# Attention in 16 steps of two query tiles in a given order, parts of queries and keys made for 128 rows at once, and rearranged ends

## The chip, the cores and the metric

One NeuronCore of a Trainium2 chip runs the kernel. Its engines work from instruction streams of their own, each in order: PE (TensorE, matrix products and transposes), DVE (VectorE), ACT (ScalarE), POOL (GpSimd) and SP (SyncE, here used to issue DMAs). The time is that of the device for one execution, in microseconds; three runs of the kernel before gave 1841.4 (median), 1840.13 (lowest) and 1842.2 (highest).

## What is computed

A decoder trunk of two layers on one sequence of 512 tokens with 1024 features, all in float32. Cut to what matters:

```python
for l in range(2):
    x = x + 0.5 * swiglu(rms_norm(x, ffn1_norm[l]), ffn1_w_in[l], ffn1_w_out[l])
    h = rms_norm(x, mix_norm[l]) @ w_mix_in[l]
    (c_x, c_b, c_c, h_q, h_f, h_i, h_g, f_q, f_k, f_v, f_f) = split(h)
    y = concatenate([
        short_conv_mixer(c_x, c_b, c_c, conv_w[l]),              # 256 columns
        hgrn2_mixer(h_q, h_f, h_i, h_g, lower_bounds[l], ...),   # 256 columns, 4 heads
        fox_mixer(f_q, f_k, f_v, f_f, fox_f_bias[l], ...),       # 512 columns, 8 heads of 64
    ])
    x = x + y @ w_mix_out[l]
    x = x + 0.5 * swiglu(rms_norm(x, ffn2_norm[l]), ffn2_w_in[l], ffn2_w_out[l])

def fox_mixer(q, k, v, f_logit, f_bias, q_gain, k_gain):         # forgetting attention
    qh = rms_norm(heads(q), q_gain) * 64 ** -0.5
    kh = rms_norm(heads(k), k_gain)
    cum = cumsum(log_sigmoid(f_logit + f_bias))
    s = qh @ kh.T + (cum[:, None] - cum[None, :])                # causal mask: -1e30
    return softmax(s) @ heads(v)
```

The hidden width of the SwiGLU is 2816.

## The kernel before

Every float32 operand of a product is split into two parts of the type fp32r: hi, a rounded copy made on ACT, and lo, the remainder made on DVE (`parted`, L337 and L338). A product is then three matrix products: hi by hi (L349), hi by lo (L355), lo by hi (L356), which add up in one bank of PSUM (`mm3`). There are eight banks under four names: `mm` (3), `sc` (2), `pt` (2) and `po` (1).

`stream_steps` is the loop for a dense projection. It takes two rows of 128 weights at a time (a granule): `granule` has SP load them into a `st` buffer (two of these), ACT and DVE make hi and lo in an `hl` buffer (three of these, hi and lo in one), and PE runs the products of all banks. Casts that run ahead (`high_priority`) are put early in the order of ACT and DVE. `wide` splits the steps of a generator in two, so that other work can be recorded between two halves; with it the first granule is taken bank by bank, else row by row, and the last one is always taken bank by bank. A line recorded through `follow` keeps its place after the line of the same engine that was recorded so before it; everything else is placed by the scheduler.

The stages of a layer:

- `ffn` (first half): `cover` runs the first columns of the input projection in steps of two column blocks (`f` = 0, 2, 4) while normalisation and a planned order of half-size products follow, then the output projection over two halves `dg`. In layer 0 `open_x` brings x in: eight pieces of 256 KB, each loaded by SP (`load_x`, L1565), transposed on PE (L1568), scaled by the gain on ACT (`norm_part`, L426) and DVE (L427). `begin_norm` (L415) loads a gain as a tile of 128 rows and 8 columns. The constants are built on DVE (L209 to L270).
- `mix`: the input projection of the three mixers. `hgrn` runs as two generators (one for each pair of heads), each `yield` of which is followed by one dense half-step of `fox_qkv` (from the third on). After the loop `fox_decay` (eight products at L1358, then `negc` at L1363 on ACT and L1364 on DVE, two parts of 8 rows) is recorded, then what is left of `fox_qkv`, 24 products of V.
- The attention, `fox_attend`: 32 items (head, tile of 128 queries). `fox_prep` makes the operands of one head: QA holds hi and lo of the queries (64 rows each), QB hi and two rows of ones, KA hi twice, KB lo and the head's two rows of `negc`. It turns queries and keys together on PE (L1419), makes the parts by two ACT operations (L1422, L1423) and two DVE operations (L1426, L1430) over 64 rows, and copies two of them by DMA on SP (L1424, L1425) from the rows where they were made to those where they belong; KB's two rows come straight from `negc` in SBUF (L1415). `scores` runs three products for an item (L1446 to L1448, the last one adds the mask in bfloat16), the row maximum on DVE, the exponential on ACT. The item's weights are turned on PE (L1510), split, and multiplied with V (`values`, L1468) once for two items. `LOOK` = 3 items of scores stand ahead. `dense` gives the short convolution's projections (`conv`) and the output projection of the six row blocks that are ready (`most`); the set `BESIDE` says beside which items one dense step is recorded.
- After the attention the last two row blocks of the output projection (`order` puts them last), and the second `ffn`. In the last layer `turn_x` (L1531, L1536) turns x back to tokens ahead of the output projection, whose banks are added to it on DVE (L510) and stored (L514).

Of the kernel before, what the change touches and what calls it, by code (L numbers as in the profile page):

```python
# [22 lines left out]
LOOK, LAG = 3, 1  # L23

BESIDE = {0, 1, 2, 33} | {4 + (29 * n) // 20 for n in range(20)}
# [158 lines left out]
class Trunk:  # L184
# [35 lines left out]
    def build_consts(self, scratch):  # L220
# [38 lines left out]
        for l in range(1, 7):  # L259
            nc.vector.tensor_scalar(a, xf, scalar1=float(2 ** (l - 1)), scalar2=None, op0=ALU.is_ge)  # L260
# [22 lines left out]
    def table(self, name):  # L283

        p = self.nc.scalar.preload_act_table_set(name)
        for user in self.tab_users:
            self.tc.add_manual_dep(p.ins, user, NOSYNC, reason="table order")
        self.tab_users = []
        self.tab = p.ins.name
# [15 lines left out]
    def granule(self, parts, kk, ahead=True, skew=0, keep=False):  # L305

        nc = self.nc
        c = sum(ap.shape[1] for ap in parts)
        st = self.wp.tile([P, 1024], F32, tag="st", name=self.n("st"), bufs=2)
        s3 = st[:, : kk * c].rearrange("p (k c) -> p k c", k=kk)
        at = 0
        for ap in parts:
            w = ap.shape[1]
            nc.sync.dma_start(s3[:, :, at : at + w], ap.rearrange("(k p) c -> p k c", p=P))
            at += w
        with self.tc.high_priority() if ahead else ExitStack():  # L320
            hi, lo = self.parted(st[:, : kk * c], 1 if ahead else kk, skew, keep)
        h3, l3 = (a.rearrange("p (k c) -> p k c", k=kk) for a in (hi, lo))
        return [(h3[:, i, :], l3[:, i, :]) for i in range(kk)]

    def parted(self, src, pieces=1, skew=0, keep=False):
# [9 lines left out]
        for c in range(0, n, w):  # L335
# [3 lines left out]
            if pieces > 1 or keep:  # L339
                self.follow("a", a)  # L340
                self.follow("v", b)
        return hh, ll
# [21 lines left out]
    def stream_steps(self, jobs, parts_of, act, nk, mid=None, pre=None, deal=None, keep=False, wide=False):  # L364
# [12 lines left out]
        while k < nk:  # L377
            kk = min(2, nk - k)
            if callable(mid) and k == nk - 2:
                mid()  # L380
            if pre is not None:
# [4 lines left out]
            rows = self.granule(parts_of(k, kk), kk, pre is None, skew, deal is not None)  # L386
            end = k + kk == nk
            order = (
                [(job, j) for job in jobs for j in range(kk)]
                if end or wide and k == 0  # L390
                else [(job, j) for j in range(kk) for job in jobs]
            )
            for n, ((acc, cols, toks, *more), j) in enumerate(order):
                if pre is not None and n == len(order) // 2:
                    pre(k, True)
                if wide and n == len(order) // 2:
# [3 lines left out]
                first, last = k + j == 0 and not more, end and j == kk - 1  # L400
                if toks is None:
                    self.mm3(acc, hi[:, cols], lo[:, cols], ah, al, first, last, False, keep)
                else:
                    self.mm3(acc, ah[:, toks], al[:, toks], hi[:, cols], lo[:, cols], first, last)
# [7 lines left out]
    def begin_norm(self, gain_ap):  # L412
# [3 lines left out]
        self.sqacc = None  # L416

# [54 lines left out]
    def ffn(self, w_in, w_out, next_gain, covered, mean=None, begin=None, out=None):  # L472
# [5 lines left out]
        with tc.tile_pool(name=self.n("ffn"), bufs=1) as fp:  # L478
# [11 lines left out]
            if last:  # L490
                xs = self.turn_x()
            for dg in range(2):
# [7 lines left out]
                self.stream(  # L500
# [5 lines left out]
                )  # L506
                if last:
                    for i in range(4):
                        o = self.xo[dg * 4 + i]
                        nc.vector.scalar_tensor_tensor(  # L510
                            out=o, in0=banks[i], scalar=0.5, in1=xs[dg * 4 + i],
                            op0=ALU.mult, op1=ALU.add,
                        )
                        nc.sync.dma_start(out[0, spans[i], dg * T : (dg + 1) * T], o)  # L514
# [11 lines left out]
    def cover(self, fp, w_in, w_out, covered, mean, begin):  # L526
# [65 lines left out]
        for f in range(0, covered, 2):  # L592
            banks = self.next4()

            def parts(k, kk, f=f):
# [9 lines left out]
                None if opening else (lambda k, f=f: deal(2 * f + k // 2)), begin is None or f > 2,  # L605
            )
# [325 lines left out]
    def mix(self, l, w, w_out, conv_w, out_gain, q_gain, k_gain, f_bias, next_gain, logits):  # L932
# [3 lines left out]
        with tc.tile_pool(name=self.n("mix"), bufs=1) as mp:  # L936
# [23 lines left out]
            def features_steps(spans, banks, mid=None):  # L960
# [3 lines left out]
                    [(b, c, None) for b, c in zip(bs, FM2)], cols(*spans), self.xact, KD, mid  # L964
# [11 lines left out]
            def tokens(*spans):  # L976
# [4 lines left out]
                    self.xact, KD, wide=True,  # L981
# [3 lines left out]
            with tc.tile_pool(name=self.n("hg"), bufs=1) as hp:  # L985
# [60 lines left out]
                self.fox_decay(mp, zf)  # L1046
                for _ in dense:
                    pass
            with tc.tile_pool(name=self.n("at"), bufs=1) as ap_:
                self.tt, self.tb = "t", 3  # L1050
# [4 lines left out]

                def conv():
                    for i in range(2):
                        bx, bc = yield from features_steps(
                            [(C_X + i * P, P), (C_C + i * P, P)], ("mm", "mm")
                        )  # L1060
                        self.conv_in(ap_, i, bx, bc, inv2, cw)
                    bb = yield from features_steps([(C_B, 256)], ("mm", "mm"))
# [6 lines left out]
                def rows(k0, a, n):  # L1069
                    return lambda k, kk: [  # L1070
                        w_out[order[k0 + k] * P : (order[k0 + k] + kk) * P, a : a + n]
                    ]
# [7 lines left out]
                def most():  # L1080

                    for dg in range(4):
# [3 lines left out]
                            rows(0, 256 * dg, 256), act(0), 6,  # L1086
# [10 lines left out]
                for n, _ in enumerate(self.fox_attend(ap_, half, qkg)):  # L1097
                    if n in BESIDE:
                        next(g)
                    if n == max(BESIDE):  # L1100
                        next(g, None)
                self.ntog = 0
                for dg in range(2):
# [3 lines left out]
                        rows(6, 512 * dg, 512), act(6), 2,  # L1107
# [36 lines left out]
    def hgrn(self, l, pr, hp, z, q, q2, v, sg, og):  # L1144
# [42 lines left out]
        self.act(kd, kd, AF.Exp)  # L1187
        tb = self.bank("pt")
# [153 lines left out]
    def fox_decay(self, mp, zf):  # L1342
# [13 lines left out]
        for j in range(4):  # L1356
# [5 lines left out]
        self.negc = mp.tile([NH, 2, T], F32R, tag="negc", name=self.n("negc"))  # L1362
        nc.scalar.activation(self.negc[:, 0, :], cb[:NH, :], AF.Copy, scale=-1.0)  # L1363
        nc.vector.scalar_tensor_tensor(  # L1364
            out=self.negc[:, 1, :], in0=cb[:NH, :], scalar=-1.0, in1=self.negc[:, 0, :],
            op0=ALU.mult, op1=ALU.subtract,
        )

# [38 lines left out]
    def fox_prep(self, pool, h, qk, g):  # L1407
# [3 lines left out]

        nc = self.nc
        tl = lambda p, tag: pool.tile([p, T], F32R, tag=tag, name=self.n(tag), bufs=2)
        QA, QB, KA, KB = tl(P, "QA"), tl(66, "QB"), tl(P, "KA"), tl(66, "KB")
        nc.sync.dma_start(KB[64:66, :].bitcast(F32), self.negc[h : h + 1, :, :].bitcast(F32))  # L1415
        nc.gpsimd.memset(QB[64:66, :].bitcast(F32), 1.0)
        b = self.bank("pt")
        for i in range(4):
            nc.tensor.transpose(  # L1419
                b[:, i * P : (i + 1) * P], qk[:, i, h % 4].rearrange("p w d -> p (w d)"), self.ident  # L1420
            )
        nc.scalar.activation(QA[:64, :], b[:64, :], AF.Copy, scale=g[:64, :])  # L1422
        nc.scalar.activation(KA[64:, :], b[64:, :], AF.Copy, scale=g[64:, :])  # L1423
        nc.sync.dma_start(QB[:64, :].bitcast(F32), QA[:64, :].bitcast(F32))  # L1424
        nc.sync.dma_start(KA[:64, :].bitcast(F32), KA[64:, :].bitcast(F32))  # L1425
        nc.vector.scalar_tensor_tensor(  # L1426
            out=QA[64:, :], in0=b[:64, :], scalar=g[:64, :], in1=QA[:64, :],
            op0=ALU.mult, op1=ALU.subtract,
        )
        nc.vector.scalar_tensor_tensor(  # L1430
            out=KB[:64, :], in0=b[64:, :], scalar=g[64:, :], in1=KA[64:, :],
            op0=ALU.mult, op1=ALU.subtract,
        )
        return QA, QB, KA, KB

    def fox_attend(self, pool, half, g):
# [3 lines left out]
        tl = lambda tag, n: pool.tile([P, T], F32, tag=tag, name=self.n(tag), bufs=n)  # L1440

        def scores(ops, i):
            QA, QB, KA, KB = ops
            c, n = slice(i * P, (i + 1) * P), (i + 1) * P
            sb = self.bank("sc")
            nc.tensor.matmul(sb[:, :n], QA[:, c], KA[:, :n], start=True, stop=False)  # L1446
            nc.tensor.matmul(sb[:, :n], QB[:, c], KB[:, :n], start=False, stop=False)
            nc.tensor.matmul(sb[:, c], self.identb, self.maskb, start=False, stop=True)  # L1448
            s1 = lambda tag: pool.tile([P, 1], F32, tag=tag, name=self.n(tag), bufs=3)
            nm, rs = s1("nm"), s1("rs")  # L1450
            nc.vector.tensor_reduce(nm, sb[:, :n], axis=AX.X, op=ALU.max, negate=True)
            pb = tl("P", 3)
            self.act(pb[:, :n], sb[:, :n], AF.Exp, bias=nm, accum_out=rs)
            nc.vector.reciprocal(rs, rs)
            if i == 3:
                nc.scalar.activation(pb[:, :n], pb[:, :n], AF.Copy, scale=rs)
            else:
                nc.vector.tensor_scalar(pb[:, :n], pb[:, :n], scalar1=rs, scalar2=None, op0=ALU.mult)
            return pb

        def values(h, i, PH, PL):
            if i == 1:
                self.ob = self.bank("po")
            t0 = (i - 1) * P
            for j in range(i + 1):
                u = 1 if j == i else 0
                for part in (PH, PL):
                    nc.tensor.matmul(  # L1468
                        self.ob[:, t0 + u * P : t0 + 2 * P],
                        half[2][:, j, h].rearrange("p a d -> p (a d)"),  # L1470
                        part[:, j, u:, :].rearrange("p i t -> p (i t)"),
                        start=j == 0 and part is PH, stop=j == i and part is PL,
                    )
            if i < 3:
# [5 lines left out]
            ft = tl("t", self.tb)  # L1480
# [7 lines left out]
        late = []  # L1488
        items = [(h, i) for h in range(NH) for i in range(4)]
        prep = lambda h: self.fox_prep(pool, h, half[h // 4], g)  # L1490
        ops = {0: prep(0)}
        yield
        pb = {it: scores(ops[0], it[1]) for it in items[:LOOK]}
        for n, (h, i) in enumerate(items):
            yield
            if i == 0 and h + 1 < NH:
                ops[h + 1] = prep(h + 1)
            if n + LOOK < len(items):
# [123 lines left out]
```

## Time and profile before

| | us |
|---|---|
| median of three runs | 1841.4 |
| the profiled execution | 1839.53 |
| its span in the trace | 1837.8 |
| PE's first instruction starts | 3.84 |
| first product of the first projection starts | 9.84 |
| DVE's last operation (L510) starts, 0.69 long | 1834.05 |

Busy time and share of each engine over stretches of layer 0's mixers (the windows of the trace), with the granted clock of PE:

| stretch, us | what runs there | PE busy | DVE busy | ACT busy | clock |
|---|---|---|---|---|---|
| 440.0 to 478.6 | end of `hgrn`, V | 38.60 | 26.35 | 21.31 | 1.00 |
| 478.6 to 484.4 | first head's operands, conv products | 5.74 | 4.20 | 3.36 | 1.00 |
| 484.4 to 500.0 | first items of the attention | 15.60 | 13.10 | 11.24 | 1.00 |
| 500.0 to 540.0 | attention with conv and output projection | 39.34 | 35.19 | 29.08 | 1.00 |
| 540.0 to 578.0 | the same | 37.58 | 30.68 | 25.83 | 1.00 |
| 578.0 to 596.0 | end of the attention | 17.78 | 13.62 | 11.44 | 1.00 |

A busy PE is the sum of its instructions' times and they are pipelined, so waits show better as distances from start to start than as idle time.

### The profile page before, as it was taken

How to read it: one execution, taken by the hardware profiler on the slowest of the kernel's cores; microseconds unless marked ns; L12 is line 12 of the kernel's file. 1: busy time of each engine (PE TensorE's matmuls, PEld its weight loads, DVE VectorE, ACT ScalarE, POOL GpSimd, SP SyncE). 2: the span in 40 equal slices, each digit the busy share in tenths (PEclk: the TensorE clock that was granted, in tenths of full speed). 3: DMA queues.
4: the chain of work that ended last, by engine and by line, in shares of the span. 5: the costliest groups of instructions: out<-in, count | busy, mean ns of one | idle time of the engine just before them, and what ended most of it. 6: DMA issues, size and time to landing. Idle time of an engine off the chain costs nothing.

```text
span 1837.8 us, 32074 instructions
## 1 busy us (share of the span) xinstructions
PE 1820.7 (99%) x12940; PEld 1668.8 (91%) x12940; DVE 1472.5 (80%) x2066; ACT 1011.6 (55%) x1446; POOL 184.9 (10%) x190
## 2 busy tenths in 40 slices
PE   8999999999999999999999999999999999999999
PEld 6899999888777899999889999998887888999997
DVE  7889787679787888879678887966778887888883
ACT  4455554465676455555445555545646665555552
POOL 0011120100000101112001111201000001020210
PEclk9999999999999999999999999999999999999999
DMA  7658783242223767868275787813313238677762
GB/s 206 184 125 192 179 178 96 69 116 69 64 75 104 211 135 171 189 167 172 81 202 138 171 190 184 170 61 90 107 52 82 75 104 229 158 153 195 153 135 92
DMA packets 245476, 253.93 MB, mean 138 GB/s; under 512 B 19632, under 2 KB 228016, under 8 KB 245328
## 3 DMA queue, kind: packets, MB, share of 16 engines
q1 hardware_dynamic: 189488, 183.69, 32.7%
q0 software_dynamic: 55840, 68.19, 23.1%
q8 instruction: 102, 1.67, 0.4%
q14 instruction: 46, 0.38, 0.1%
HBM read 226.08 MB, written 2.10 MB: 124 GB/s over the span
## 4 chain that ended last, share of the span: by engine, by line
PE 92%; DVE 4%; ACT 2%; issue 1%; DMA 1%; SPq 0%; ACTq 0%; DVEq 0%
PE mm L349 13%; PE mm L356 13%; PE mm L355 13%; PE sc L349 6%; PE sc L356 6%; PE sc L355 6%; PE pt L349 6%; PE pt L355 6%; PE pt L356 6%; PE po L349 4%; PE po L355 4%; PE po L356 4%; DVE hl L338 1%; ACT hl L337 1%; PE sc L1297 1%
## 5 line engine op out<-in xcount | busy, mean ns | idle before, releaser
L738 ACT CAST hl<-w 128x1024 fp32r<-128x1024 f32 x322 | 337.7, 1050 | 345.8 <-PE mm L356 81.7
L740 DVE TENSOR_TENSOR hl<-w,hl 128x1024 fp32r<-128x1024 f32 x322 | 392.7, 1221 | 87.6 <-ACT hl L738 87.4
L338 DVE TENSOR_TENSOR hl<-st,hl 128x1024 fp32r<-128x1024 f32 (+2 forms) x172 | 162.9, 949 | 131.5 <-ACT hl L337 131.0
L337 ACT CAST hl<-st 128x1024 fp32r<-128x1024 f32 (+2 forms) x172 | 142.0, 829 | 180.9 <-PE po L356 71.7
L349 PE MATMUL mm<-xc,hl 128*128 128x256 f32 (+1 forms) x730 | 201.3, 276 | 0.3 <-ACT g L837 0.3
L356 PE MATMUL mm<-xc,hl 128*128 128x256 f32 x728 | 201.2, 276 | 0.0
L355 PE MATMUL mm<-xc,hl 128*128 128x256 f32 x728 | 201.1, 276 | 0.0
L349 PE MATMUL sc<-xc,hl 128*128 128x256 f32 (+1 forms) x530 | 146.3, 277 | 0.6 <-ACT g L837 0.6
L356 PE MATMUL sc<-xc,hl 128*128 128x256 f32 x528 | 146.1, 277 | 0.0
L355 PE MATMUL sc<-xc,hl 128*128 128x256 f32 x528 | 146.0, 276 | 0.0
L349 PEld LDWEIGHTS mm<-xc,hl 128*128 128x128 f32 x730 | 137.1, 188 | 0.8 <-ACT g L837 0.5
L356 PEld LDWEIGHTS mm<-xc,hl 128*128 128x128 f32 x728 | 136.7, 188 | 0.1
L355 PEld LDWEIGHTS mm<-xc,hl 128*128 128x128 f32 x728 | 136.7, 188 | 0.0
L355 PE MATMUL pt<-xc,hl 128*128 128x256 f32 x480 | 132.6, 276 | 0.0
L349 PE MATMUL pt<-xc,hl 128*128 128x256 f32 (+1 forms) x482 | 132.6, 276 | 0.0
L356 PE MATMUL pt<-xc,hl 128*128 128x256 f32 x480 | 132.5, 276 | 0.0
L349 PE MATMUL mm<-x,hl 128*128 128x512 f32 x272 | 109.5, 402 | 0.0
L355 PE MATMUL mm<-x,hl 128*128 128x512 f32 x272 | 106.5, 391 | 0.0
L356 PE MATMUL mm<-x,hl 128*128 128x512 f32 x272 | 106.4, 391 | 0.0
L349 PEld LDWEIGHTS sc<-xc,hl 128*128 128x128 f32 x530 | 99.5, 188 | 1.5 <-ACT g L837 1.0
L356 PEld LDWEIGHTS sc<-xc,hl 128*128 128x128 f32 x528 | 99.2, 188 | 0.1
L355 PEld LDWEIGHTS sc<-xc,hl 128*128 128x128 f32 x528 | 99.1, 188 | 0.0
(470 smaller groups left out, 5510.4 us busy)
## 6 DMA issues: line engine op xcount, KB each, us to landing
w<-in_ffn_w_in_dram SPq DMA_DIRECT2D x140, 512.0 KB
w<-in_ffn_w_out_dram SPq DMA_DIRECT2D x64, 512.0 KB
w<-in_ffn_w_out_dram POOLq DMA_DIRECT2D x56, 512.0 KB, 9.3
w<-in_ffn_w_in_dram POOLq DMA_DIRECT2D x39, 512.0 KB, 8.0
st<-in_ffn_w_in_dram SPq DMA_DIRECT2D x72, 256.0 KB
st<-in_w_mix_in_dram SPq DMA_DIRECT2D x72, 256.0 KB
w<-S POOLq DMA_DIRECT2D x35, 512.0 KB, 4.7
st<-in_ffn_w_out_dram SPq DMA_DIRECT2D x24, 512.0 KB
```

What stands on the lines that cost most here:

```text
L337: a = nc.scalar.copy(hi, src[:, c : c + w])
L338: b = nc.vector.tensor_sub(lo, src[:, c : c + w], hi)
L349: i = nc.tensor.matmul(acc[:, c], ah, bh[:, c], start=first and c.start == 0, stop=False, skip_group_check=True,)
L355: nc.tensor.matmul(acc, ah, bl, start=False, stop=False, skip_group_check=True)
L356: i = nc.tensor.matmul(acc, al, bh, start=False, stop=last, skip_group_check=True)
L738: A(nc.scalar.copy(hi, src))
L740: return lambda: V(nc.vector.tensor_sub(lo, src, hi))
L1297: nc.tensor.matmul(s2[:, :, t], e[:, i * P : (i + 1) * P], e2[:, :, t], start=True, stop=True)
```

## The change

It has these parts:

- **Start.** The gain is loaded as 8 rows of 128 and turned by PE. The first granule is loaded from ACT's queue, a row and a span at a time, ahead of the load of ACT's table, the pieces of x follow each other on SP, and the constants of DVE stand behind the first parts. The second row's scaling (`between`) stands between the parts of the two rows.
- **`lead`, `fine`, `deep`, `rowwise`, `last`** replace `wide`: the first granule by banks (`lead`, also for `f` = 2), two halves of a step (`fine`), granules of `deep` rows (4 for the short convolution, 3 for the output projection beside the attention), the last granule by rows (`rowwise`), and the last bank in two halves of 256 columns (`last`).
- **hgrn** gets a `yield` ahead of the transposes at L1190.
- **`fox_decay`** writes `negc` to DRAM, from where each head's two rows are read.
- **`fox_prep`** makes hi by one ACT operation and lo by one DVE operation over 128 rows, then puts them in place by six DMAs on SP.
- **`fox_attend`** has 16 steps of two tiles of queries (tiles 0 and 1, then 2 and 3), in an order kept by `follow`: the transposes of a step's weights, the scores of two steps ahead, the values of the step before, the operands of the head two ahead. A step's two masks are added by one product for tiles 0 and 1. `BESIDE` now gives the number of dense half-steps after each step.
- **End.** `turn_x` runs as a generator, four pieces beside each granule step.

```diff
-BESIDE = {0, 1, 2, 33} | {4 + (29 * n) // 20 for n in range(20)}
+BESIDE = (2, 1, 1) + (1, 1, 1, 1, 1, 1, 2) + (2, 1, 2, 2, 2, 2, 1, 2, 2)
...
             if pre is not None:
+                if k == 0:
+                    st = self.load_rows(parts_of(k, kk), kk, self.nc.scalar)
+                    self.table(LNEXP)
+                    self.follow("a", self.tab_ins)
                 pre(k)
...
-                if end or wide and k == 0
+                if end and not rowwise or lead and k == 0
...
+            if halves:
+                acc, cols, toks = jobs[-1]
+                for c in (slice(0, T // 2), slice(T // 2, T)):
...
-        nc.sync.dma_start(self.gain, gain_ap.rearrange("(k p) -> p k", p=P))
+        g = pool.tile([KD, P], F32, tag="S", name=self.n("gr"), bufs=2)
+        self.follow("s", nc.sync.dma_start(g, gain_ap.rearrange("(k p) -> k p", p=P)))
+        b = self.bank("pt")
+        self.follow("p", nc.tensor.transpose(b[:, :KD], g, self.ident[:KD, :KD]))
+        self.follow("v", nc.vector.tensor_copy(self.gain, b[:, :KD]))
...
+                lead=f == 2 and begin is not None,
...
         self.act(kd, kd, AF.Exp)
+        yield
         tb = self.bank("pt")
...
+        self.negc = self.dram.tile([NH, 2, T], F32, tag="negc", name=self.n("negc"))
+        nc.sync.dma_start(self.negc, negc.bitcast(F32))
...
-        nc.scalar.activation(QA[:64, :], b[:64, :], AF.Copy, scale=g[:64, :])
-        nc.scalar.activation(KA[64:, :], b[64:, :], AF.Copy, scale=g[64:, :])
-        nc.sync.dma_start(QB[:64, :].bitcast(F32), QA[:64, :].bitcast(F32))
-        nc.sync.dma_start(KA[:64, :].bitcast(F32), KA[64:, :].bitcast(F32))
...
+        hi, lo = (tl(P, self.tt, self.tb) for _ in range(2))
+        nc.scalar.activation(hi, b, AF.Copy, scale=g)
+        nc.vector.scalar_tensor_tensor(
+            out=lo, in0=b, scalar=g, in1=hi, op0=ALU.mult, op1=ALU.subtract
+        )
+        for to, src in (
+            (QA[:64], hi[:64]), (KA[:64], hi[64:]), (KA[64:], hi[64:]), (QB[:64], hi[:64]),
+            (QA[64:], lo[:64]), (KB[:64], lo[64:]),
+        ):
+            nc.sync.dma_start(to.bitcast(F32), src.bitcast(F32))
...
+        prep(0)
+        yield
+        scores(0, 0)
+        prep(1)
+        yield
+        scores(0, 1)
+        yield
+        for k, (h, p) in enumerate(steps):
+            turn(h, p)
+            if k + 2 < len(steps):
+                scores(*steps[k + 2])
+            if k:
+                values(*steps[k - 1])
+            if p == 0 and h + 2 < NH:
+                prep(h + 2)
             yield
+        values(*steps[-1])
```

More of the change, by code (lines that the diff above doesn't have):

```diff
@@ L341, in parted @@
                 self.follow("v", b)
+            if pieces > 1 and c == 0:
+                self.between()
         return hh, ll
@@ L505, in ffn @@
                     parts, lambda k: (self.hh[k // 2][:, k % 2, :], self.hl[k // 2][:, k % 2, :]), nf,
-                )
+                    last=last and dg == 1,
+                ):
+                    if last:
+                        next(turn, None)
                 if last:
@@ L1054, in mix @@
                 nc.scalar.activation(inv2, inv, AF.Square)
+                beside = dict(keep=True, fine=True, deep=4)
                 def conv():
@@ new lines, in turn @@
+        def turn(h, p):
+            to = weights.pop((h, p))
+            blocks = [(j, u) for j in range(2 * p + 2) for u in range(2) if j <= 2 * p + u]
+            PH, PL = (
+                pool.tile([P, 7, P], F32R, tag=t_, name=self.n(t_), bufs=2) for t_ in ("PH", "PL")
+            )
+            for a in range(0, len(blocks), 4):
+                some = blocks[a : a + 4]
+                tb = self.bank("pt")
+                for k, (j, u) in enumerate(some):
+                    E(nc.tensor.transpose(
+                        tb[:, k * P : (k + 1) * P], to[u][:, j * P : (j + 1) * P], self.ident
+                    ))
+                ph, pl = (x[:, a : a + len(some), :].rearrange("p b t -> p (b t)") for x in (PH, PL))
+                t = tb[:, : len(some) * P]
+                nc.scalar.copy(ph, t)
+                nc.vector.tensor_sub(pl, t, ph)
+            turned[h, p] = blocks, PH, PL
@@ L1463, in values @@
+        def values(h, p):
+            blocks, PH, PL = turned.pop((h, p))
+            if p == 0:
                 self.ob = self.bank("po")
-            t0 = (i - 1) * P
-            for j in range(i + 1):
-                u = 1 if j == i else 0
+            last = 2 * p + 1
+            for j in range(last + 1):
+                at = [k for k, (jj, _) in enumerate(blocks) if jj == j]
+                o = slice((2 * p + 2 - len(at)) * P, (2 * p + 2) * P)
                 for part in (PH, PL):
[L1468 to L1473, printed above, removed]
@@ L1474, in values @@
-            if i < 3:
+                    E(nc.tensor.matmul(
+                        self.ob[:, o], V[:, j, h].rearrange("p a d -> p (a d)"),
+                        part[:, at[0] : at[-1] + 1, :].rearrange("p b t -> p (b t)"),
+                        start=j == 0 and part is PH, stop=j == last and part is PL,
+                        skip_group_check=True,
+                    ))
+            if p == 0:
                 return
```

254 lines of the change are left out of this document (139 added, 115 removed).

## The prediction

> **What bounds the kernel now.** I read the page's busy shares first, then its chain of work that ended last, then the waits of PE.
>
> ```profile
> PE 1820.7 (99%) x12940; PEld 1668.8 (91%) x12940; DVE 1472.5 (80%) x2066; ACT 1011.6 (55%) x1446; POOL 184.9 (10%) x190
> ...
> PE 92%; DVE 4%; ACT 2%; issue 1%; DMA 1%; SPq 0%; ACTq 0%; DVEq 0%
> ...
> PE mm L1568 <- DMA xs<-in_x_dram: 6.5, 2, 3.8
> PE pt L1190 <- ACT t L292: 1.9, 2, 1.2
> PE po L349 <- DVE nt L448: 0.8, 1, 0.8
> PE sc L1531 <- ACT xt L1536: 0.5, 1, 0.5
> ```
>
> PE (TensorE) is busy 99% and is 92% of the chain. A change gains only by removing PE work or one of PE's few stops; it loses whatever new stop it makes. PE work: the distances from start to start of products in the trace (227 ns for 512 columns, 170 for 384, 113 for 256, 57 for 128, 109 for a transpose of 128, some 87 more on the first product behind a transpose) multiplied over the built order of either kernel give 1781.1 us before and 1781.8 after. So the change takes no PE work away; everything below is stops. The sum is made against the profiled execution (1839.53 us, span 1837.8), which is 1.9 below the median 1841.4.
>
> **Opening.** The timeline of the first microseconds (start, duration, engine, line; idle time and its releaser at the end):
>
> ```profile
> 3.84 1.94 PE L1568 MATMUL mm<-ident,xs 128*128 128x128 f32 x8 [3.84 <-DMA xs<-in_x_dram]
> 5.91 0.17 DVE L638 TENSOR_SCALAR ngain<-gain 128x8 f32<-128x8 f32 x1 [2.85 <-DMA gain<-in_ffn_norm_dram]
> 8.42 1.11 PE L1568 MATMUL mm<-ident,xs 128*128 128x128 f32 x4 [2.64 <-DMA xs<-in_x_dram]
> 9.84 0.78 PE L349 MATMUL sc<-x,hl 128*128 128x512 f32 x1
> 10.41 0.63 PE L355 MATMUL sc<-x,hl 128*128 128x512 f32 x1
> 10.84 0.63 PE L349 MATMUL sc<-x,hl 128*128 128x512 f32 x1
> ```
>
> The first product starts at 9.84, behind the third piece of x (transposes at 8.42), which stands in SP's queue behind the gain and two loads of weight rows. After: x0 to x2 stand first on SP, the first weight rows go out on ACT's queue in four DMAs, the gain comes as 8 rows and is turned by PE. Before, x0 and x1 are used at 3.84 and about 4.6, so a piece of 256 KB takes 0.8 to 0.9 us; x2 then lands at 5.4, or up to 1.0 later if the rows of ACT's queue share the engines. With the rest of the chain as before (8.42 to 9.84 is 1.4) the first product starts at 6.8 to 7.8; the built order puts only two of x2's transposes ahead of it, so I take 6.8: −3.0. Bounds: −1.0 if landings at 0.9 us for each 256 KB stay the limit (x, weights: the same bytes), −4.1 if the 0.7 to 1.1 us that PE waits between the first two pairs of rows, behind DVE's constants, go too.
>
> **f = 2 (`lead`).** PE's stop of 1.0 us at 38.75 (the po row of the waits) waits for DVE's nt to free the bank; in the new order that bank comes 18 products later (18 x 0.227 = 4.1 us). −1.0; nothing else moves.
>
> **hgrn's extra `yield`.** PE waits for `kd` before L1190's transposes once a layer: start to start 1.36 and 0.85 us over the pitch. A dense half-step (12 products, 2.7 us) goes between. −2.2 in both layers together. Its price is in the next part: the loop now uses up all 24 half-steps of `fox_qkv`, where before two of them (24 products x 0.227 = 5.45 us) were left to run behind `fox_decay`.
>
> **First scores of the attention, the term that decides.** Before:
>
> ```profile
> 478.63 0.60 PE L1419 MATMUL pt<-ident,qk 128*128 128x128 f32 x4
> ...
> 478.89 0.61 ACT L337 CAST hl<-st 128x512 fp32r<-128x512 f32 x1
> ...
> 479.98 0.68 ACT L1422 ACTIVATE QA<-pt,qkg 64x512 fp32r<-64x512 f32 x1
> ...
> 480.68 0.68 ACT L1423 ACTIVATE KA<-pt,qkg 64x512 fp32r<-64x512 f32 x1
> ...
> 481.42 0.58 SPq L1425 DMA_DIRECT2D KA<-KA  x1
> ...
> 482.23 0.76 DVE L1430 SCALAR_TENSOR_TENSOR KB<-pt,qkg,KA 64x512 fp32r<-64x512 f32 x1
> ...
> 484.31 0.30 PE L1446 MATMUL sc<-KA,QA 128*128 128x128 f32 x1
> ```
>
> The head's transposes stand at 478.63, ACT has its parts from 479.98, two DMAs follow, and the scores at 484.31 come 0.23 late: the chain is just covered by 24 conv products. The last packet of KA lands at 483.95, 2.5 us after its issue at 481.42; an issue takes 0.55 to 0.58 of SP.
>
> After, the same 24 conv products lie between the transposes and the scores, but ACT's order there is: negc (L1434), hy, a cast of 1024 columns (L357), `iv2` (L1120), and only then the head's part (L1497). That cast needs the hl buffer that those very 24 products read: it waits for the last of them. ACT is in order, so the head's part stands behind. From the end of the products (t = 0): cast 0.2 + 1.05 (row of L738: 1050 ns), iv2 0.63, hi 0.68: 2.6. Then SP issues four DMAs of hi, 4 x 0.55, and the fifth (QA's lower half, from lo) starts at 4.8, lands at 4.8 + 2.5 = 7.3; the sixth (KB, needed by the second product) 0.5 later. DVE's chain is the second bound: behind two hgrn tails, four V parts, the 1.23 us subtractions and negc it has 14.3 us of work from about 4 us before `fox_decay`'s end, so lo ends 10.3 after that end, and some 2 us later if the ten or so crossings between ACT and DVE in it cost 0.2 each; that is 4.4 to 6.4 after the products (which end 5.9 after `fox_decay`), and with an issue and a landing (3.0) 7.4 to 9.4. So PE stops 7.3 to 9.4; I take 8.4, less 0.2 of before: +8.2 a layer. Both layers have the same order: **+16.4**. Behind the waiting scores stands all of PE, and ACT's and DVE's softmax. negc's way over DRAM (a write and a read on SP) is earlier and hidden: at negc's end SP has nothing else; if that cover goes, the read is one more landing, about 2.5, already inside the upper end.
>
> The clock after such a stop has no row of its own in mid-kernel. The nearest is the opening: after 2.64 us without work PE's first products start 0.43 us apart (10.41, 10.84, then up to 12.97) instead of 0.227, which costs 7 steps x 0.2 = 1.5. Bounds 0 and 1.5 a stop, 3.0 in both layers; softmax and not PE limits what follows the stop, and the granted clock is 1.00 in all windows, so I take 0 in the sum and the other end as a rival.
>
> **Heads 1 to 7.** A head's parts now take one ACT and one DVE operation over 128 rows for four over 64 (about 0.7 each), but seven DMAs for three, 7 x 0.55 = 3.9 us of SP in a head of 9.7 to 12 us. The order gives a head two steps of lead, about 9.7 us; its chain (0.44 transposes, 0.7, 0.7, 5 x 0.55, 2.5) is 7. PE's stops over its pitches between 484.4 and 578 add up to about 4.2 a layer now. I take −0.5 a layer, −1.0; bounds −4.1 a layer (all gone) and +3.
>
> **The ends.** The row-wise order of `rowwise` puts the last head's values' users later: the stops of 0.34, 0.11, 0.06, 0.21, 0.11 between 580 and 589: −0.8 a layer, −1.7. `turn_x` between the products: 0.71 + 0.17 + 0.17 at 1797.7 to 1801: −1.1. The last bank in halves: both halves' DVE operations wait for the very last product in the built order, so only the smaller last operation and DMA count: −0.2 (bounds −0.6, +0.2). Casts of deep granules (1050 ns for 1024 columns against two of 0.62) unload ACT and DVE beside a busy PE: 0, and in their cover nothing is lost if it goes, as they are shorter in sum.
>
> **Sum:** −3.0 − 1.0 − 2.2 + 16.4 − 1.0 − 1.7 − 1.1 − 0.2 = +6.2, 1845.7 in the profiled execution, **1847.6** at the median.
>
> **The rivals.**
> 1. The clock falls after each stop: +3.0, 1850.6. For it: the opening's 0.43 us. Against: it needs a stop of several us, which the chain gives, but ACT and DVE may limit the products behind it. The Trainium skill ("TensorE: Matmul & The Clock Gate", section "HAM oscillation — how this bites in real kernels") says that no gap over about 3.4 us should be left on PE, since the next products then start at half clock; the opening's distances agree with it, no run here shows it in mid-kernel.
> 2. The other side: the stop at the first scores lets ACT and DVE get ahead, and no later head waits: heads −8.2 instead of −1.0, opening −4.1, stop at its low end (7.1 a layer, −2.2): 1847.6 − 7.2 − 1.1 − 2.2 = 1837.1, faster. For it: ACT and DVE stand idle during the stop except for work of later steps. Against: they too are in order, and what follows them needs the same scores. It decides from the point where heads 1 to 7 wait under 0.1 us each.
> 3. SP's queue makes every head late: seven issues in order, each head's last landing 1.3 behind its scores, 6 heads x 1.3 x 2 = 15.6: 1847.6 + 1.0 + 15.6 = 1864.2. For it: KA landed just in time with two DMAs. Against: 3.9 of 9.7 us.
> 4. The opening does not do what it says, bound by landings: −1.0 for −3.0: 1849.6.
>
> **How the numbers follow.** Chances: forecast 0.36 (1844 to 1852), clock 0.26, other side 0.2, queue 0.08, opening 0.1. About 0.2% (3.7 us) can be told from no change: faster is under 1837.7, slower over 1845.1. Faster: most of rival 2, 0.17; same: the rest of it and the low tail of the forecast, 0.18; slower 0.65. Range: from rival 2 to the clock's case with the stop at 9.4: 1836 to 1857; the likeliest alone 1843 to 1852.
>
> **What would show it.** The first score product of head 0 preceded by 7 to 9 us of idle PE in both layers, with the cast (L357) starting at the last conv product's end and iv2 and hi behind it; if that stop is under 2 us the forecast is wrong and the kernel is faster. First product near 6.8; L1190 without idle; no 1.0 us stop near 36; products behind the stop at 0.227 or 0.43.

## The result, and the profile after

The changed kernel took 1860.34 us in the median of four runs (1858.6 to 1861.48), the kernel before 1841.26 beside it: 1.0105 times as long, 95% interval 1.0093 to 1.0117. The direction was forecast, the size was not: +19.1 us for +6.2, and 1860.3 lies above the range's end of 1857.

The profile page of the changed kernel (busy time, chain that ended last, waits of PE):

```profile
PE 1826.8 (98%) x12931; PEld 1676.9 (90%) x12931; DVE 1447.7 (78%) x1968; ACT 999.9 (54%) x1410; POOL 184.7 (10%) x190
...
PE 89%; DVE 5%; ACT 3%; issue 1%; DMA 1%; SPq 0%; DVEq 0%; ACTq 0%
```

```profile
PE sc L1533 <- issue: 7.4, 1, 7.4
PE sc L1533 <- DMA QA<-t: 7.2, 1, 7.2
PE mm L1677 <- DMA xs<-in_x_dram: 2.8, 3, 2.3
PE mm L371 <- ACT fyh L1605: 2.4, 2, 1.2
...
PE sc L1368 <- DVE t L1326: 1.0, 2, 0.5
PE sc L1368 <- DVE fr L506: 1.0, 2, 0.5
```

PE is still the chain, with two stops of over 7 us that were not there: the first scores of head 0, once in each layer. `issue` in the first row only means that the profile names no releaser. L1190 and the `po` row of `f` = 2 are gone from the list; a wait for `fyh` and two rows of L1368 (inside `hgrn`) have come.

Where the time went can be read without any model, from the same instructions in both traces (start to start, us; the difference adds up to the 20.5 between the last products):

| from ... to | before | after | difference |
|---|---|---|---|
| start to the norm's sum behind `f` = 0 | 35.15 | 33.87 | −1.3 |
| to the sum of layer 0's mixer norm | 315.53 | 315.75 | +0.2 |
| to head 0's transposes | 127.95 | 128.73 | +0.8 |
| to the first scores | 5.68 | 13.29 | +7.6 |
| to the last `values` | 101.15 | 102.05 | +0.9 |
| to the sum of the next norm | 27.83 | 28.29 | +0.5 |
| to layer 1's mixer norm | 644.14 | 644.99 | +0.9 |
| to head 0's transposes | 127.38 | 128.24 | +0.9 |
| to the first scores | 5.52 | 13.50 | +8.0 |
| to the last `values` | 101.17 | 102.62 | +1.4 |
| to the sum of the next norm | 27.83 | 28.27 | +0.4 |
| to the last product | 314.29 | 314.47 | +0.2 |

The stop in layer 0, by the timelines of PE, ACT and SP of the changed kernel (start, duration, engine, line):

```profile
478.35 0.61 PE L1493 MATMUL pt<-ident,qk 128*128 128x128 f32 x4
...
484.07 0.39 PE L378 MATMUL mm<-x,hl 128*128 128x512 f32 x1
491.64 0.45 PE L1533 MATMUL sc<-KA,QA 128*128 128x128 f32 x1 [7.18 <-DMA QA<-t]
```

```profile
483.58 0.62 ACT L1409 CAST hy<-t 128x512 fp32r<-128x512 f32 x1 [3.56 <-DVE t L1406]
484.50 1.04 ACT L357 CAST hl<-st 128x1024 fp32r<-128x1024 f32 x1 [0.29 <-PE mm L378]
...
485.98 0.67 ACT L1497 ACTIVATE t<-pt,qkg 128x512 fp32r<-128x512 f32 x1
```

```profile
486.67 0.47 SPq L1505 DMA_DIRECT2D QA<-t  x1
...
489.17 0.54 SPq L1505 DMA_DIRECT2D QA<-t  x1
```

The last of the 24 products starts at 484.07; ACT's cast starts right behind it, `iv2` and the head's part follow, then six DMAs one after the other. The fifth (QA) starts at 489.17 and the scores 2.47 later. That is the chain of the forecast, instruction for instruction. A second gate stands just beside the first: the attention's tiles lie in memory that `hgrn` used. DVE's last operation on it (L1410) ran from 484.23 to 484.92, and SP's first load for KB (at 485.07) and ACT's `iv2` wait for it. So without the cast the head's part would have started little earlier; this is read from the trace, the two gates were not tried apart.

Behind the stop the granted clock falls. Windows of the changed kernel (us; busy time and instructions of PE, PEld, DVE, ACT, POOL; granted clock; DMA share; GB/s), the last row from layer 1:

```profile
476.00:484.00 8.00, 8.00 (x42) 6.24 (x41) 7.97 (x13) 4.26 (x8) 0.00 (x0) 1.00 0.25 73
484.50:491.50 7.00, 0.00 (x0) 0.00 (x0) 2.34 (x3) 2.15 (x3) 0.98 (x2) 0.84 0.48 110
491.50:493.90 2.40, 2.14 (x9) 1.92 (x10) 0.29 (x1) 0.12 (x1) 0.00 (x0) 0.50 0.78 230
...
496.10:500.00 3.90, 3.90 (x20) 2.96 (x19) 1.59 (x4) 1.61 (x4) 0.52 (x1) 1.00 0.89 202
...
1408.70:1414.20 5.50, 5.42 (x17) 4.51 (x18) 2.09 (x6) 1.60 (x5) 0.00 (x0) 0.50 0.47 136
```

In layer 0 PE runs at half clock for 4.5 us (491.6 to 496.1), products 0.43 us apart, in layer 1 for 5.5. Set against the same instructions at a clock of 1.00 (layer 0 of the second run below), this costs 2.0 and 2.5 us. They are in the table's rows from the first scores to the last `values`.

### The profile page after: what moved, and what is told of

Same layout as the page of the kernel before. It is cut to its first block, busy times and chain, and to the rows that moved or that the text cites. A ratio compares the mean times of both kernels' runs of the same rounds, so it can differ in the third digit from the quotient of the medians.

```text
span 1858.3 us, 32027 instructions
## 1 busy us (share of the span) xinstructions
PE 1826.8 (98%) x12931; PEld 1676.9 (90%) x12931; DVE 1447.7 (78%) x1968; ACT 999.9 (54%) x1410; POOL 184.7 (10%) x190
## 4 chain that ended last, share of the span: by engine, by line
PE 89%; DVE 5%; ACT 3%; issue 1%; DMA 1%; SPq 0%; DVEq 0%; ACTq 0%
PE mm L371 12%; PE mm L378 12%; PE mm L377 12%; PE sc L371 6%; PE sc L378 6%; PE sc L377 6%; PE pt L371 6%; PE pt L377 6%; PE pt L378 6%; PE po L371 3%; PE po L377 3%; PE po L378 3%; DVE hl L358 1%; PE sc L1533 1%; PE po L1588 1%
## 5 line engine op out<-in xcount | busy, mean ns | idle before, releaser
L358 DVE TENSOR_TENSOR hl<-st,hl 128x1024 fp32r<-128x1024 f32 (+3 forms) x152 | 160.1, 1054 | 149.6 <-ACT hl L357 149.3
L357 ACT CAST hl<-st 128x1024 fp32r<-128x1024 f32 (+3 forms) x152 | 138.6, 912 | 169.2 <-PE po L378 84.0
```

What stands on the lines that cost most here:

```text
L357: a = nc.scalar.copy(hi, src[:, c : c + w])
L358: b = nc.vector.tensor_sub(lo, src[:, c : c + w], hi)
```

## The experiments

Each is compared with the kernel before on the same chip. Stops are distances from start to start over the usual pitch.

**Undo the yield.**

```diff
         self.act(kd, kd, AF.Exp)
-        yield
         tb = self.bank("pt")
```

> The changed kernel without the new yield ahead of L1190. Theory (the loop of hgrn uses up the 24 products of V that covered the first head's operands): two half-steps of V run behind fox_decay again, 5.45 us, so the stop ahead of the first scores falls from 7.3 to about 2 us in each layer, stays too short to bring the granted clock to 0.50 (2.2 us a layer), and the stops at L1368 that came with the yield (1.7 us a layer) go; the stops ahead of L1190 (1.36 and 0.85) come back. Sum: -10.7 - 4.4 - 3.4 + 2.2 = -16.3 against the changed kernel, about 1844. Rival (six DMAs on SP and the way of negc over DRAM make the operands late, whatever lies before): the stop moves with the work ahead and stays 6 us or more; only the L1368 and L1190 terms change, about 1858.

Measured: 1848.81 (1844.53 to 1850.73), 1.0041 times the kernel before (1.0027 to 1.0055); −11.5 against the changed kernel. The stop fell from 7.4 to 3.4, not to 2, and the clock still fell behind it. The trace is of the slowest execution (granted clock 0.996 on the whole); two of the five took 1844.5 and 1844.7, at 0.998 and 0.999, close to what was expected, so the median holds a part of the clock's loss. The L1368 rows went and L1190's came back. Half of the theory: cover matters most, but something else is late by another 1.5 us.

**Keep the yield, start the dense half-steps later**, so that two of them (24 products of V) are left behind `fox_decay`.

```diff
                         step += 1
-                        if step > 2:
+                        if step > 4:
                             next(dense, None)
```

> The changed kernel with the yield, but the dense half-steps beside hgrn begin at its fifth step for the third. Theory: two half-steps are left behind fox_decay as in the run without the yield, so the same -10.7 - 4.4 at the first scores, and L1190 keeps its cover; what it costs is cover at hgrn's start, 0 to 5 us a layer. About 1845 to 1853. Rival (the late operands are SP's or negc's): the stop stays at 6 us or more, 1858 to 1865.

Measured: 1845.12 (1842.92 to 1848.31), 1.0026 times before (1.0016 to 1.0035). Stops of 3.3 and 3.5 us ahead of the scores; the waits of L1190 and of L1368 are both gone: from the mixer norm's sum to head 0's transposes 126.52 and 126.50 us for 127.95 and 127.38 before, −1.4 and −0.9, the sizes that the forecast gave to the yield. Windows of this run, the stop and what follows it, first layer 0, then layer 1:

```profile
481.00:484.70 3.70, 0.61 (x3) 0.19 (x1) 1.23 (x1) 1.04 (x1) 0.00 (x0) 1.00 0.88 231
484.70:488.00 3.30, 3.21 (x18) 2.74 (x19) 1.49 (x4) 1.52 (x5) 0.00 (x0) 1.00 0.53 159
```

```profile
1390.00:1394.00 4.00, 0.69 (x4) 0.23 (x3) 1.22 (x1) 1.04 (x1) 0.00 (x0) 1.00 0.79 215
1394.00:1397.00 3.00, 2.97 (x13) 2.67 (x14) 1.28 (x3) 1.60 (x5) 0.00 (x0) 0.64 0.60 180
```

Two stops of nearly one length: the clock stays at 1.00 behind the first and falls to 0.64 behind the second.

ACT's part was done at 478.48, 3 us before the products ended; then SP took 3.7 us for six issues (478.53 to 482.23), and the scores started at 484.77.

**The old operands for all heads**: `fox_prep`'s body as before (two ACT and two DVE operations over 64 rows, two DMAs), the rest changed.

> The changed kernel with the old fox_prep: two ACT and two DVE operations over 64 rows, two DMAs for six (negc still over DRAM). Theory (the operands start late, behind a cast that waits for the last of the 24 products): the start of the head's first ACT part stays 1.4 us behind the last product; four issues of 0.55 to 0.6 fall away, so the stop goes from 7.3 to about 5 us, still long enough for the clock to fall. -4.5 for both layers, and for the heads behind it -1 to +4. About 1855 to 1859. Rival (the six DMAs are the cause): the stop goes under 1.5 us and the clock stays at 1.00, -16, about 1844.

Measured: 1866.65 (1866.4 to 1867.03), 1.0143 times before (1.0128 to 1.0158), 6.3 slower than the changed kernel. The stop fell to 5.6 and 5.5, as the theory had it, but the heads behind paid 6 us a layer, for −1 to +4 expected. Some 1.5 of the 6 is the clock's, estimated from the time at half clock: it fell a second time in each layer, behind stops of 1.8 and 2.0 us. Waits of PE in this run:

```profile
PE sc L1535 <- DMA KA<-KA: 10.7, 2, 5.4
PE pt L1572 <- DVE KB L1504: 9.2, 6, 1.8
```

The new order of the attention needs the operations over 128 rows: with the old ones the transposes of the weights wait 9.2 us for DVE.

**One half-step moved behind the copies of heads 2 and 3.**

```diff
-... + (2, 1, 2, 2, 2, 2, 1, 2, 2)
+... + (1, 1, 3, 2, 2, 2, 1, 2, 2)
```

> The changed kernel with one dense half-step moved from the step ahead of values(3,1) to two steps later, (1, 1, 3, ...) for (2, 1, 2, ...) in the last part of BESIDE. Theory: the stop of 2.1 us a layer at 549 and 1466 (PE's first product of fyh waits for the copies L1605 and L1606 of heads 2 and 3) comes from the dense products reaching these rows one half-step too early: it goes, -4.2, about 1856. Rival (ACT and DVE limit the steps there, whatever PE has to do): the stop moves to the next transposes, the time stays at 1860.

Measured: 1856.8 (1855.76 to 1857.88), −3.5 of the 4.2 expected; the wait for `fyh` is gone and some of it stands at the next transposes.

**Late start, and the old operands for head 0 alone**: the second run's edit, and the old body behind `if h == 0`.

> The changed kernel with the dense half-steps beside hgrn from its fifth step on, and with the old fox_prep (two DMAs) for head 0 alone; heads 1 to 7 keep the new one. Theory: of the stop of 3.3 us that is left ahead of the first scores, four DMA issues of 0.6 and the later start of the last two landings are most; with two DMAs the operands land some 2.5 to 3 us earlier, the stop is 0 to 0.8 us in both layers and the granted clock stays at 1.00 behind it. -5 to -6.6, and -1 for the clock's loss in some executions: 1838 to 1840, from 1845.1. Rival (ACT's order, with V and iv2 ahead of the head's part, is what is late): the stop stays at 2.5 us or more, 1843 to 1845.

Measured: 1840.11 (1837.76 to 1842.77), 0.9995 times before (0.9986 to 1.0004), the clock at 1.00 in the profiled run. The gain is there, but the stop is still 2.3 us, so its reason was only half right. SP's rows of layer 0:

```profile
478.54 0.40 SPq L325 DMA_DIRECT2D st<-in_w_mix_in_dram  x1
478.98 0.51 SPq L1499 DMA_DIRECT2D QB<-QA  x1
479.67 0.46 SPq L1500 DMA_DIRECT2D KA<-KA  x1
```

KA's last packet lands 4.3 us after its issue, for 2.5 in the kernel before. Ahead of it on the queue is a load of 512 KB of weights (granules of four rows), whose packets run from 479.6 to 482.1.

**The same with the moved half-step.**

> The run before with the dense half-step of BESIDE moved behind the copies of heads 2 and 3. Theory: its gain (3.5 of 1860.3 measured alone) adds to the others: 1834.5 to 1836.5, faster than the kernel before. Rival (stops of one layer share a cause, and the gain is taken by the next wait): 1838 to 1840.

Measured: 1840.14 (1837.74 to 1840.93), no gain over the run before it: the rival's time, but not for its reason. In the profiled run the products behind the stop lost 1.6 us in each layer to a low clock, against the same products at 1.00 in the run before (a stop of 2.2 sufficed). Where the clock stays at 1.00 with the moved half-step, in the profile of the next run, the first scores to the last `values` take 98.94 us in both layers, for 99.99 and 100.54 without it: the half-step gains 1.0 to 1.6 a layer, and the clock took it back. Why the clock fell here and not in the run before stays open.

**Row-wise or bank by bank at the end**: the run above without `rowwise`.

> The run before with the last two row blocks of the output projection taken bank by bank again in both halves. Theory (the row-wise order reaches the second row, fyh of the last heads, 1.4 us after the first, before its copy is made: stops of 0.24 and 0.50 at 596 for 0.21 before): bank by bank reaches it even earlier, at 0.7 us, so the row-wise order is right and taking it away costs 0.5 to 1.5 us for both layers. Rival (the row-wise order itself made the end worse by 0.45 a layer, as the totals of the stages read): -0.9.

Measured: 1843.88 (1841.27 to 1846.51), +3.7; the stage behind the last `values` waits 3.1 us for 1.05 in each layer. Of the two kept orders the row-wise one is right. It is still 0.45 a layer longer than before, and not because the copies of the last heads end later: in both kernels that of `fyh` starts 2.5 us and that of `fyl` 3.1 us behind the start of the last product of `values`. The kernel before ran its end by rows too, as the scheduler had placed it, and took three products of `fyh` ahead of the first of `fyl`; in the order that is now kept the product of `fyl` comes second and waits for its copy. First two rows of the kernel before, then one of the changed kernel:

```profile
588.62 0.74 PE L349 MATMUL sc<-fyh,hl 128*128 128x512 f32 x2
...
589.44 0.41 PE L355 MATMUL sc<-fyl,hl 128*128 128x512 f32 x1
```

```profile
597.57 0.50 PE L377 MATMUL sc<-fyl,hl 128*128 128x512 f32 x1 [0.22 <-DVE fyl L1606]
```

From the product ahead of it, that one starts 0.72 us later, for a pitch of 0.23.

**The first rows on SP's queue.**

```diff
-                    st = self.load_rows(parts_of(k, kk), kk, self.nc.scalar)
+                    st = self.load_rows(parts_of(k, kk), kk, self.nc.sync)
```

> The changed kernel with the first weight rows on SP's queue ahead of x for ACT's queue beside it. Theory (the start is bound by the bytes that have to land, 512 KB of rows and 768 KB of x ahead of the first product, whichever queue): first product at 7.9 to 8.6 as in the changed kernel. Rival (ACT's queue moves the rows beside x at no cost): the three pieces of x land 1.8 us later, first product at 9.5 or later, about +1.7 on the whole.

Measured: 1858.8 in one run; the first product at 8.53 for 7.91 in the changed kernel and 8.08 to 8.82 in the runs with its opening. One run, but it agrees with a start bound by what has to land, not by the queue. In the changed kernel PE's rows say the same:

```profile
4.81 1.11 PE L1677 MATMUL mm<-ident,xs 128*128 128x128 f32 x4 [2.29 <-DMA xs<-in_x_dram]
6.26 1.11 PE L1677 MATMUL mm<-ident,xs 128*128 128x128 f32 x4 [0.34 <-DMA xs<-in_x_dram]
...
7.91 0.78 PE L371 MATMUL sc<-x,hl 128*128 128x512 f32 x1
```

Pieces of x are used 1.4 us apart where they were 0.9 apart without rows beside them.

**Three half-steps ahead of head 0's scores**, on top of the run with the moved half-step.

```diff
-BESIDE = (2, 1, 1) + (1, 1, 1, 1, 1, 1, 2) + (1, 1, 3, 2, 2, 2, 1, 2, 2)
+BESIDE = (3, 1, 1) + (1, 1, 1, 1, 1, 1, 1) + (1, 1, 3, 2, 2, 2, 1, 2, 2)
```

> The run with old operands for head 0 and the moved half-step, and three dense half-steps for two between head 0's transposes and its scores (one less later). Theory: the 2.2 us that are left ahead of the first scores are covered by the 12 products more (2.7 us): stop 0 to 0.5 in both layers, the granted clock stays at 1.00 behind it; -4.4 and -1.4 for the clock: 1834 to 1836, faster than the kernel before by 5. Rival (ACT takes the cast and the conv copies ahead of the head's part, so the operands move back with the products): stop of 1.5 or more, 1839 to 1841.

Measured: 1830.17 (1829.48 to 1831.4), 0.9936 times before (0.9922 to 0.9949): faster than both kernels, and by more than expected. The stop is 0.05 us in both layers and the clock stays:

```profile
481.00:484.10 3.10, 3.10 (x17) 2.56 (x15) 1.23 (x1) 1.05 (x1) 0.00 (x0) 1.00 0.40 120
484.00:488.00 4.00, 4.00 (x24) 3.41 (x22) 2.09 (x6) 2.10 (x6) 0.00 (x0) 1.00 0.60 164
```

**Head 0's two DMAs on ACT's queue**, two half-steps ahead of the scores: `nc.scalar.dma_start` for `nc.sync.dma_start`.

> The run with old operands for head 0 and the moved half-step, its two DMAs issued by ACT for SP. Theory (KA's rows land 4.3 us after their issue for 2.5 since a load of 512 KB of weights, issued 0.4 us earlier on the same queue, is ahead of them in the DMA engines): a queue of its own lets the head's packets pass between the weights': stop of 2.2 falls to about 1; -2.4, 1837 to 1838. Rival (the engines share their time whatever the queue): the stop stays at 2.

Measured: 1839.23 (1837.47 to 1841.34), 0.9984 times before (0.9975 to 0.9993); stops of 2.5 and 2.0 us for 2.2 and 2.35. The rival: from ACT's queue KA's last packet still lands 4.4 and 4.0 us after its issue, so another queue did not bring these packets past the weights'.

**Granules of two rows in the short convolution.** This kernel records only 28 of the 40 dense half-steps and so leaves out 12 of the 16 of the output projection beside the attention; its time can't be set beside the others.

> The same run with granules of two rows for four in the short convolution's projections. Theory: the load ahead of the head's DMAs is 64 KB for 512 KB and the stop of 2.2 us goes to 0.3 or less; the casts of 512 columns for 1024 cost ACT and DVE 0.2 and 0.15 us a half-step more, hidden or up to 2 us in all. 1835 to 1838. Rival (the order of ACT, not the load, holds the operands): the stop stays at 2 and the casts cost 1 to 3: 1841.

Measured: 1819.04, of no use as a time. Its first scores come 5.2 us after head 0's transposes for 8.1 with granules of four, behind half as many products; the stop itself stays at 2.0. KA lands 2.3 us after its issue there, for 4.3, with a load of 128 KB ahead of it (64 in the expectation) for 512. That fits the load as the cause of the long landing, but the order of the casts has changed with it; it is not shown.

**Two numbers alone**: the changed kernel's operands for every head, with the late start and the `BESIDE` of the run with three half-steps.

> The changed kernel with its new operands for every head, and only the places of dense half-steps changed: beside hgrn from the fifth step, three for two ahead of head 0's scores, and the one ahead of values(3,1) moved. Theory (cover is all that was missing): of the 3.3 us stop that is left with the late start, 2.7 are covered, 0.6 a layer stays, the clock stays at 1.00: 1830.2 + 1.2 = 1831.4, 1830.5 to 1833. Rival (the six DMAs need the old operands for head 0 in any case): the landings move back behind the loads that the extra half-step brings, stop of 2 or more, 1835 to 1838.

Measured: 1833.06 (1831.94 to 1834.75), 0.9959 times before (0.9945 to 0.9972). Stops of 0.5 and 0.95 us, the clock at 1.00. The places of some half-steps, with no line of the attention touched, take the changed kernel from 19.1 us slower than before to about 7.6 faster.

## Why the prediction was right in kind and wrong in size

The stop that was to decide came, by the steps that were forecast. Two other terms of the sum failed most: the clock behind the stop, put at 0, cost 4.5 us, and `hgrn`'s yield, put at −2.2, came to +1.7.

- **The stop at the first scores**: right, with the instructions, the queue and the engine named; +16.4 forecast, +15.6 measured (7.6 and 8.0). Taking back the cover that the yield had eaten (two half-steps, 5.45 us) and giving 2.7 more removed it; six DMAs and a 512 KB load ahead in the queue set how much cover is needed. Of the forecast's two bounds SP's held (7.3 from the products' end to the scores, as in the trace). DVE's, which gave the upper end of 9.4, did not: lo ended 3.2 us behind the products (487.49), for 4.4 to 6.4; a crossing from ACT to DVE that was put at 0.2 took 0.03 there (L357's end at 485.54, L358's start at 485.57). That the negc read over DRAM costs nothing here was argued, not tried.
- **The clock behind it**: the step that failed most. The forecast set it to 0 in the sum, since the granted clock was 1.00 in all windows of before, and gave 1.5 a stop to a rival. It fell in both layers, and cost 2.0 and 2.5: +4.5. The windows of before could not speak for it: they hold no stop of that kind. The only one that did was the opening's, and 1.5 was read from it at a stop of 2.6 us. That reading was wrong: ahead of that stop PE was slow already (the eight transposes from 3.84 take 1.94 us, where 0.109 each would be 0.87), so the opening shows a start at half speed and not a fall, and the windows' granted clock of 1.00 does not tell it. The rule of the Trainium skill ("TensorE: Matmul & The Clock Gate", section "HAM oscillation — how this bites in real kernels") that stood as the rival was right here.
- **hgrn's yield**: −2.2 forecast, +1.7 measured. The L1190 stops went as forecast, but the same half-steps reach `hgrn`'s later products (L1368) one earlier, and PE then waits there for DVE (1.7 us over the pitch in layer 0); the forecast counted the wait that was covered and not the ones that this would bring. What makes DVE late there was not tried alone. With a later start (second run) the full −2.3 appears.
- **Heads 1 to 7**: −1.0 forecast. The rows from the first scores to the last `values` are +0.9 and +1.4, and without the clock's 2.0 and 2.5 −1.1 each, although a new stop of 2.1 a layer for `fyh` is in them. Right, a little small. The old operands in the new order cost 6 a layer, so the new order needs the new ones; the new operands in the old order were not tried.
- **The ends**: `turn_x` went as forecast (the waits of L1531 are gone). `f` = 2: −0.75 for −1.0. The end of the attention: −1.7 forecast, +0.9 measured: only the old stops were priced. The order by rows, from which the gain was to come, was there before, and keeping it set the product of `fyl` ahead of its copy. The opening: −3.0 forecast, −1.3 measured, near the bound of −1.0 for landings (rival 4); in the profiles of the other runs with this opening the same row takes 33.6 to 35.0, so about 1 us of it is chance.
- **Noise of one trace**: 3.2 of the 20.5 are stretches of slower products that come and go between executions (below), three in this profile and none in that of before. The medians differ by 19.1 with them averaged over.

The terms missed add up: clock 4.5, hgrn 3.9, ends 2.6, opening 1.7 and slow stretches 3.2, less 2.0 by which stop and heads came out better, are 13.9 of the 14.3 between 20.5 and 6.2. The range was too narrow because each small term was taken at its good end while only the stop had both bounds kept. Its own terms, the clock's case with a stop of 9.4, come to 1852.6 (1850.6 and twice 1.0) and not to the 1857 that stands there; the rest of it has no term.

## What to carry to other kernels

When a wait is covered by work that was already there, ask what that work was covering before, and look for the first instruction behind it that now has nothing in front of it. A stop on the bounding engine can cost more than its length: those of 7 us brought the clock down in both layers, for another 2.0 and 2.5 us, and some of about 2 us did, for another 1.4 to 1.6, so price the two together and remove the stop whole. Before rewriting a chain that ends late, try moving independent work in front of it: moving half-steps by two constants was worth 27 us here (1860.3 to 1833.1).

## What the runs showed of the hardware

- The clock falls after stops shorter than expected, and not always. Behind 7.2 us it fell in both layers; behind 3.3 to 3.5 in one layer of two with the late start (windows above) and in both without the yield; behind 2.2 in both layers of this run:

```profile
481.80:484.10 2.30, 0.35 (x2) 0.00 (x0) 0.84 (x1) 1.04 (x1) 0.00 (x0) 1.00 0.47 140
484.10:488.80 4.70, 4.66 (x19) 3.83 (x20) 2.48 (x7) 1.51 (x5) 0.00 (x0) 0.69 0.62 165
```

This is the run with old operands for head 0 and the moved half-step. Without the moved half-step the same stops (2.35 and 2.2) left it at 1.00 in both layers. In the run without the yield it fell even behind a stop of 1.2 us with one of 0.5 right behind it, the wait for `fyh` in layer 1:

```profile
1459.80:1463.20 3.40, 3.40 (x13) 2.79 (x14) 2.00 (x5) 1.06 (x2) 0.00 (x0) 0.50 0.89 203
```

The same two stops in the changed kernel left it at 1.00, so the length of a stop does not decide alone; what else does stays open. The Trainium skill ("TensorE: Matmul & The Clock Gate", the section named above) puts the gap to be avoided at some 3.4 us; here 2.2 and less were enough, in some executions.

- Products of 256 columns run 113.3 ns apart, but in some stretches 117.8, with the granted clock at 1.00. In the changed kernel such a stretch runs from 1201 on, where the products' starts are 1201.59, 1201.71, 1201.83 and 1201.95. It begins behind one product that is late by 0.1 us, lasts to the next change of shape (some 25 us) and costs about 1 us. The traces of this case hold none to three of them, always at one of the same four places in the feed-forward parts but not in every execution. What sets them off stays open.
